# Convolution sums in PSUM, one-hots from columns of biases, and candidates' places spread by ScalarE in a hybrid decoder layer

## The chip, the cores and the metric

The kernel runs on one core of a Trainium2 chip. The metric is device time in microseconds, the median over runs. The kernel before took 3189.76, 3202.34 and 3205.40 us in three runs, median 3202.34 us.

## The reference, cut to what matters

One decoder layer over 1024 tokens of 1024 numbers in f32: attention and a convolution beside each other, then a retrieval among 128 x 128 single-neuron experts (8 heads, 16 experts each per token), then a per-layer embedding behind a gate.

```python
def _token_mixers(xn, ...):                       # attention: left out
    glu = a * jax.nn.sigmoid(gt)
    c = lax.conv_general_dilated(glu, conv_w[:, None, :], window_strides=(1,),
                                 padding=[(CONV_WIDTH - 1, 0)], ...,      # 31 taps, causal
                                 feature_group_count=D_CONV) + conv_b     # 512 channels, each its own
    c = jax.nn.silu(_layernorm(c, conv_ln_g, conv_ln_b))
    ...

def _peer(xn, w_q, sub_keys, expert_u, expert_v):
    q = (xt @ w_q).reshape(N, PEER_HEADS, 2, D_KEY // 2)
    s = jnp.einsum('nhpc,pkc->nhpk', q, sub_keys)
    s_half, i_half = lax.top_k(s, PEER_TOPK)                  # 16 of 128 keys in each half
    cand = (s_half[:, :, 0, :, None] + s_half[:, :, 1, None, :]).reshape(N, PEER_HEADS, 256)
    top_s, top_c = lax.top_k(cand, PEER_TOPK)                 # the places of the best 16 candidates
    i1 = jnp.take_along_axis(i_half[:, :, 0], top_c // PEER_TOPK, axis=-1)
    i2 = jnp.take_along_axis(i_half[:, :, 1], top_c % PEER_TOPK, axis=-1)
    expert = i1 * N_KEYS + i2
    gate = jax.nn.softmax(top_s, axis=-1)
    h = jnp.einsum('td,tkd->tk', xb, expert_u[eb])            # per block of tokens
    act = jax.nn.gelu(h, approximate=False) * gb
    return jnp.einsum('tk,tkd->td', act, expert_v[eb])
```

## The kernel before, in words

**Groups and tiles.** The 1024 tokens are eight tiles of 128, taken in four groups of two. For each group the program goes through norm and projections, attention and convolution (`convolve`), output projection and the next norm, search among the keys, and the choice among candidates. Tiles 0, 1, 6 and 7 find their experts by fetching rows: GpSimd issues an indirect transfer per row number (line 593, six buffers), VectorE multiplies each row of `u` with the token's vector (line 606, 512 rows) and later adds each row of `v` to the sum (line 622, 512 rows). Tiles 2 to 5 go another way: `gate_matrix` builds for each token a matrix of gates over all 128 x 128 experts, writes it to DRAM, and a dense pass (`dense`, lines 700 to 772) runs over every expert with the products split into high and low parts. Eight closing blocks, one for each tile, apply the embedding and the final norm.

**What sets the order.** The program names no order among the engines beyond its data: a scheduler lays out each engine's queue when the program is built, from the dependences, the buffers and the order in the text. The row steps of lines 593, 606 and 622 have no fixed place and are laid between the other steps on GpSimd and VectorE. A queue is then executed in order. The rows of VectorE's queue between two fixed points thus differ from one program to the next.

**The convolution.** A group has four channel tiles of 128 channels by 256 tokens (`c` = 0 to 3). For each, the gated input `glu` is made from two projections (line 335) that lie in PSUM under the tag `lin`. This tag has three buffers of one bank and is shared by all projections, by the transposed convolution output `pc` and by the products of `gate_matrix`. Of the 31 taps, 16 (`SIDE_TAPS`) are products on ScalarE (line 349), which GpSimd adds up in `side` (line 350, 15 additions for each channel tile). The other 15 run on VectorE: line 353 begins the sum `cc` in SBUF, line 356 is 14 multiply-adds on it, and line 357 adds `side`. There are two buffers of `side`, three of `glu` and five of `cc`.

**The candidates' places.** For each tile the places of the 16 chosen candidates (`p16`, 8 heads of 16) are split into the two numbers `i1` and `i2`. VectorE compares every place with 16 constants (line 555, `ge`, bf16, 128 partitions of 2048), where `p16` is read as a broadcast over its last dimension, multiplies and adds up (lines 557 to 566), and compares again with 16 constants (line 569, `eq`). After that, in VectorE's order, come the first norm and the attention of the next group.

**The gate matrices.** Per tile, 32 quads of four tokens. For each quad VectorE makes a one-hot `oa` of the first number times the gate (line 669) out of a difference that TensorE builds in PSUM by two products (`less_keys`, lines 654 and 655). The one-hot `o2` of the second number is made in two ways by turns: in every second quad VectorE compares with `iota`, in the others TensorE builds the difference by the same two products and ScalarE applies an absolute value (line 675) and a ramp `1 - x` cut at zero (line 676). TensorE then multiplies the two for each token (line 679), ScalarE copies the result to a stage (line 680), and SyncE writes a stage of 2 MB to DRAM.

## Time and profile before

| | before |
|---|---|
| three runs | 3189.76, 3202.34, 3205.40 us |
| profiled execution | 3194.15 us |
| span in the trace | 3192.4 us |
| mean granted TensorE clock | 0.940 |
| TensorE (PE) busy | 2774.8 us, 87%, 11839 instructions |
| TensorE weight loads (PEld) | 2011.9 us, 63% |
| VectorE (DVE) busy | 2589.0 us, 81%, 5116 instructions |
| ScalarE (ACT) busy | 1089.5 us, 34%, 1917 instructions |
| GpSimd (POOL) busy | 1539.5 us, 48%, 1268 instructions |
| HBM | 270 GB/s over the span |

The profiled execution is 1.75 us longer than the span of its trace, from the first instruction to the last, and all sums of durations are made within that one execution. Shares of busy time are averages over very different stages: a share of 87% says that TensorE works most of the time, not that it is the limit everywhere. So the stages are looked at one by one, by busy time in stretches of the span. SyncE issues transfers and is not counted as busy. In the views, "idle before, releaser" is the time an engine stood still ahead of an instruction, and what ended it.

### The profile page before, as it was taken

The numbers are of one execution on the slowest core, as the hardware profiler recorded it, in microseconds if no ns is written. First come the engines' busy times: TensorE is split into PE (matmuls) and PEld (weight loads), VectorE is DVE, ScalarE is ACT, GpSimd is POOL, SyncE is SP. The second block draws the span as 40 slices with busy tenths as digits, with TensorE's granted clock in tenths as the row PEclk, the third lists the DMA queues.
The fourth block names the chain that finished last, engine by engine and source line by source line (L and its number), as shares of the span: only waits on it lengthen the run. The fifth ranks groups of instructions, "written<-read, shape, count | busy, mean of one in ns | idle before, by whom it ended". The sixth has DMA issues, their size and how long they took to land. (4 is left out here: it accounts for less than half of the span.)

```text
span 3192.4 us, 36241 instructions
## 1 busy us (share of the span) xinstructions
PE 2774.8 (87%) x11839; PEld 2011.9 (63%) x11839; DVE 2589.0 (81%) x5116; ACT 1089.5 (34%) x1917; POOL 1539.5 (48%) x1268
## 2 busy tenths in 40 slices
PE   6688959968994859995999999999999999999996
PEld 3465625743673545664777777777777777777643
DVE  1728887998899898886888888888889888988861
ACT  2722443363245225662222222222322322222342
POOL 0501585455536521223665565565556566666530
PEclk9898979978997879997999999999999999999998
DMA  4154859718843846989999999999999999999850
GB/s 163 53 177 159 270 193 345 266 53 315 305 164 106 329 152 213 290 259 345 342 347 334 323 343 347 339 337 362 328 341 329 334 354 345 358 330 338 326 209 23
DMA packets 304528, 865.77 MB, mean 271 GB/s; under 512 B 26778, under 2 KB 93746, under 8 KB 304338
## 3 DMA queue, kind: packets, MB, share of 16 engines
q0 software_dynamic: 147456, 536.94, 46.1%
q1 hardware_dynamic: 153616, 323.16, 29.2%
q10 hardware_dynamic: 3266, 3.36, 0.3%
q8 instruction: 93, 1.52, 0.2%
q14 instruction: 97, 0.79, 0.1%
HBM read 819.83 MB, written 43.52 MB: 270 GB/s over the span
## 5 line engine op out<-in xcount | busy, mean ns | idle before, releaser
L593 POOL DMA_INDIRECT u<-in_expert_u_dram,ex x512 | 666.7, 1302 | 825.0 <-DVE hk L606 484.7
L593 POOL DMA_INDIRECT v<-in_expert_v_dram,ex x512 | 676.7, 1322 | 522.9 <-DVE gy L622 377.3
L622 DVE SCALAR_TENSOR_TENSOR gy<-v,ga,gy 128x1024 f32<-128x1024 f32 x512 | 656.7, 1283 | 52.0 <-DMA v<-in_expert_v_dram,ex 42.7
L606 DVE CUSTOM_DVE_ANT_0 u<-u,gxn 128x1024 f32<-128x1024 f32 x512 | 617.7, 1233 | 37.5 <-DMA u<-in_expert_u_dram,ex 36.8
L735 PE MATMUL ph<-xh,uh 128*128 128x512 f32 x1024 | 404.9, 395 | 40.4 <-ACT uh L711 39.6
L737 PE MATMUL ph<-xh,ul 128*128 128x512 f32 x1024 | 406.5, 397 | 25.4 <-DVE ul L713 25.0
L736 PE MATMUL ph<-xl,uh 128*128 128x512 f32 x1024 | 402.3, 393 | 0.0
L753 ACT CAST vh<-v 128x1024 fp32r<-128x1024 f32 x128 | 131.5, 1052 | 759.3 <-PE kept_y L768 517.0
L350 POOL TENSOR_TENSOR side<-side,tap 128x256 f32<-128x256 f32 x240 | 195.9, 818 | 183.8 <-ACT tap L349 170.1
L735 PEld LDWEIGHTS ph<-xh,uh 128*128 128x128 f32 x1024 | 194.5, 190 | 88.4 <-ACT uh L711 48.0
L737 PEld LDWEIGHTS ph<-xh,ul 128*128 128x128 f32 x1024 | 194.1, 190 | 79.4 <-DVE ul L713 39.5
L755 DVE TENSOR_TENSOR vl<-v,vh 128x1024 fp32r<-128x1024 f32 x128 | 154.0, 1222 | 108.7 <-ACT vh L753 105.0
L766 PE MATMUL py<-vh,ah 128*128 128x512 f32 x512 | 204.4, 399 | 40.5 <-ACT ah L745 40.5
L270 PE MATMUL pq<-x2T,w_pq 128*128 128x256 f32 x1024 | 229.8, 383 | 2.7 <-DMA w_pq<-in_peer_wq_dram 1.6
L736 PEld LDWEIGHTS ph<-xl,uh 128*128 128x128 f32 x1024 | 194.6, 190 | 41.2
L270 PEld LDWEIGHTS pq<-x2T,w_pq 128*128 128x128 f32 x1024 | 193.9, 192 | 30.6 <-ACT pqT L480 3.2
L767 PE MATMUL py<-vl,ah 128*128 128x512 f32 x512 | 200.7, 394 | 0.0
L766 PE MATMUL kept_y<-vh,ah 128*128 128x512 f32 x512 | 199.5, 390 | 0.0
L768 PE MATMUL kept_y<-vh,al 128*128 128x512 f32 x512 | 199.5, 390 | 0.0
L767 PE MATMUL kept_y<-vl,ah 128*128 128x512 f32 x512 | 199.3, 389 | 0.0
L768 PE MATMUL py<-vh,al 128*128 128x512 f32 x512 | 198.3, 395 | 0.3 <-DVE al L747 0.3
L711 ACT CAST uh<-u 128x1024 fp32r<-128x1024 f32 x128 | 134.1, 1048 | 110.0 <-DMA u<-in_uT_dram 82.3
(261 smaller groups left out, 4796.5 us busy)
## 6 DMA issues: line engine op xcount, KB each, us to landing
u<-in_uT_dram SPq DMA_DIRECT2D x128, 512.0 KB
v<-in_expert_v_dram SPq DMA_DIRECT2D x128, 512.0 KB
w_pq<-in_peer_wq_dram SPq DMA_DIRECT2D x64, 512.0 KB
gate_d<-stage SPq DMA_DIRECT2D x16, 2048.0 KB
gt<-gate_d SPq DMA_DIRECT2D x64, 512.0 KB
w_o<-in_w_out_dram SPq DMA_DIRECT2D x32, 512.0 KB
w_k<-in_w_qkv_dram SPq DMA_DIRECT2D x16, 512.0 KB
w_q<-in_w_qkv_dram SPq DMA_DIRECT2D x16, 512.0 KB
```

The lines of the kernel that those rows point to most:

```text
L270: nc.tensor.matmul(a, w[:, k, :], xT[:, k, :], start=k == 0, stop=k == KD - 1)
L350: G.tensor_tensor(side, side, m, ALU.add)
L593: d = G.indirect_dma_start(out=e, out_offset=None, in_=table, in_offset=bass.IndirectOffsetOnAxis(ap=index, axis=0))
L606: uses(V.tensor_tensor_reduce(out=e, in0=e, in1=xn, scale=1.0, scalar=0.0, op0=ALU.mult, op1=ALU.add, accum_out=hk[:, k : k + 1]))
L622: uses(V.scalar_tensor_tensor(y, e, act[:, k : k + 1], y, ALU.mult, ALU.add))
L735: nc.tensor.matmul(ph, hi, xh[:, k, :], start=k == 0, stop=False)
L736: nc.tensor.matmul(ph, hi, xl[:, k, :], start=False, stop=False)
L737: nc.tensor.matmul(ph, lo, xh[:, k, :], start=False, stop=k == KD - 1)
L755: V.tensor_tensor(b, v, a.bitcast(F32), ALU.subtract)
L766: nc.tensor.matmul(py, ah[e][:, rows(j)], vh[e][:, half(f)], start=first, stop=False)
L767: nc.tensor.matmul(py, ah[e][:, rows(j)], vl[e][:, half(f)], start=False, stop=False)
L768: nc.tensor.matmul(py, al[e][:, rows(j)], vh[e][:, half(f)], start=False, stop=last_e)
```

## The change

It has three parts. First, the convolution's sum on VectorE is held in a PSUM buffer of the tag `lin` (`cs`, for sums) in place of SBUF, and only the last addition, now line 358, writes the SBUF tile `cc`. Second, ScalarE copies `p16`, broadcast, into the full bf16 tile, and VectorE's two comparisons read that tile and write it in place. Third, a negated copy `i2N` of the transposed second numbers is made, and in every second quad ScalarE builds the difference by four activations over `iota`, one for each token, with a column of `i2N` as bias and the absolute value as function; the two products of TensorE for that quad are gone.

```diff
--- before.py
+++ after.py
@@ -348,13 +348,14 @@
                     m = apool.tile([P, GN], F32, tag="tap", name=f"tap{g}_{c}_{k}", bufs=2)[:, :gn]
                     S.activation(m, xk, AF.Copy, scale=wk)
                     G.tensor_tensor(side, side, m, ALU.add)
-            cc = apool.tile([P, GN], F32, tag="cc", name=f"cc{g}_{c}", bufs=5)[:, :gn]
+            sums = lin(f"cs{g}_{c}")[:, :gn]
             xk, wk = tap(SIDE_TAPS)
-            V.tensor_scalar(cc, xk, wk, cw[:, c, TAPS : TAPS + 1], ALU.mult, ALU.add)
+            V.tensor_scalar(sums, xk, wk, cw[:, c, TAPS : TAPS + 1], ALU.mult, ALU.add)
             for k in range(SIDE_TAPS + 1, TAPS):
                 xk, wk = tap(k)
-                V.scalar_tensor_tensor(cc, xk, wk, cc, ALU.mult, ALU.add)
-            V.tensor_tensor(cc, cc, side, ALU.add)
+                V.scalar_tensor_tensor(sums, xk, wk, sums, ALU.mult, ALU.add)
+            cc = apool.tile([P, GN], F32, tag="cc", name=f"cc{g}_{c}", bufs=5)[:, :gn]
+            V.tensor_tensor(cc, sums, side, ALU.add)
             cT.append(cc)
         return cT
 
@@ -552,7 +553,8 @@
         bcast_k = lambda a: a.unsqueeze(2).to_broadcast(full)
         const = lambda o: cb16[:, o : o + TOPK].unsqueeze(1).unsqueeze(1).to_broadcast(full)
         ge = big("ge")
-        V.tensor_tensor(ge, p16.unsqueeze(3).to_broadcast(full), const(0), ALU.is_ge)
+        S.copy(ge, p16.unsqueeze(3).to_broadcast(full))
+        V.tensor_tensor(ge, ge, const(0), ALU.is_ge)
 
         step = mpool.tile([P, PH, TOPK], BF16, tag="step", name=f"step{nm}")
         V.tensor_copy(step[:, :, 0:1], ix4[:, :, 0, 0:1])
@@ -566,7 +568,8 @@
         total(st, ge)
         V.tensor_tensor(p16, p16, st, ALU.subtract)
         eq = big("eq")
-        V.tensor_tensor(eq, p16.unsqueeze(3).to_broadcast(full), const(2 * TOPK), ALU.is_equal)
+        S.copy(eq, p16.unsqueeze(3).to_broadcast(full))
+        V.tensor_tensor(eq, eq, const(2 * TOPK), ALU.is_equal)
         V.tensor_tensor(eq, eq, bcast_k(ix4[:, :, 1, :]), ALU.mult)
         i2 = mpool.tile([P, PH, TOPK], BF16, tag="i2", name=f"i2{nm}", bufs=ND + 1)
         total(i2, eq)
@@ -646,6 +649,8 @@
             S.copy(d, pt[:, 0:P])
             tr.append(d)
         i2T, gT = tr
+        i2N = gp.tile([P, P], F32, tag="i2N", name=f"i2N{j}", bufs=2)
+        S.activation(i2N, i2T, AF.Copy, scale=-1.0)
         four = [P, 4, NK]
 
         def less_keys(ix, t0, name):
@@ -672,7 +677,8 @@
                     )
                 else:
 
-                    S.activation(o2, less_keys(i2, t0, f"pd2_{j}_{t0}"), AF.Abs)
+                    for e in range(4):
+                        S.activation(o2[:, e, :], iota, AF.Abs, bias=i2N[:, t0 + e : t0 + e + 1])
                     S.activation(o2, o2, AF.Relu, bias=1.0, scale=-1.0)
                 pg = sps(f"pG{j}_{t0}")
                 for e in range(4):
```

The scheduler lays the queues out anew. Three places follow, before and after; a name is buffer, group, channel tile and a running number, so `cc1_3` is the sum of channel tile 3 in group 1, and a number at the end of a tile's name differs between the two programs.

VectorE at the end of the convolution of group 1, before. `r_mix2` is the reciprocal for the norm of group 2, and `u0_31` the row number 31 of `u` for tile 0:

```order
L356 SCALAR_TENSOR_TENSOR cc1_3_2558<-glu1_3_2315,cw_91,cc1_3_2558 128x256
L356 SCALAR_TENSOR_TENSOR cc1_2_2494<-glu1_2_2287,cw_91,cc1_2_2494 128x256
L356 SCALAR_TENSOR_TENSOR cc1_3_2558<-glu1_3_2315,cw_91,cc1_3_2558 128x256
L153 RECIPROCAL r_mix2_2586<-sd_mix2_2584 128x2
L153 RECIPROCAL r_ya1_2788<-sd_ya1_2786 128x2
L356 SCALAR_TENSOR_TENSOR cc1_3_2558<-glu1_3_2315,cw_91,cc1_3_2558 128x256
L334 COPY glu2_0_3862<-last_100 128x30
L606 ISA u0_31_18830,hk0_18734<-u0_31_18830,gxn0_18735 128x1024
```

After:

```order
L356 SCALAR_TENSOR_TENSOR cs1_2_2504<-glu1_2_2295,cw_91,cs1_2_2504 128x256
L356 SCALAR_TENSOR_TENSOR cs1_3_2569<-glu1_3_2323,cw_91,cs1_3_2569 128x256
L356 SCALAR_TENSOR_TENSOR cs1_2_2504<-glu1_2_2295,cw_91,cs1_2_2504 128x256
L356 SCALAR_TENSOR_TENSOR cs1_3_2569<-glu1_3_2323,cw_91,cs1_3_2569 128x256
L358 TENSOR_TENSOR cc1_2_2520<-cs1_2_2504,side1_2_2457 128x256
L358 TENSOR_TENSOR cc1_3_2585<-cs1_3_2569,side1_3_2522 128x256
L153 RECIPROCAL r_mix2_2598<-sd_mix2_2596 128x2
L153 RECIPROCAL r_ya1_2800<-sd_ya1_2798 128x2
L334 COPY glu2_0_3874<-last_100 128x30
L334 COPY glu2_1_3902<-last_100 128x30
L334 COPY glu2_2_3930<-last_100 128x30
L609 ISA u0_36_18885,hk0_18774<-u0_36_18885,gxn0_18775 128x1024
```

Before, the last tap steps of channel tile 3 lie behind `r_mix2`, between row steps; after, both chains of the pair and their last additions come ahead of it, and the rows 31 to 35 have gone earlier.

GpSimd in group 1, before, from the fourth channel tile's first additions (`side1_3`) on; `u0_41` and so on are fetches:

```order
L350 TENSOR_TENSOR side1_3_2511<-side1_3_2511,tap1_3_1_2513 128x256
L593 DMA u0_41_18860<-in_expert_u_dram,ex0_1846 128x1024
L350 TENSOR_TENSOR side1_3_2511<-side1_3_2511,tap1_3_2_2516 128x256
L593 DMA u0_42_18863<-in_expert_u_dram,ex0_1846 128x1024
L350 TENSOR_TENSOR side1_3_2511<-side1_3_2511,tap1_3_3_2519 128x256
L593 DMA u0_43_18866<-in_expert_u_dram,ex0_1846 128x1024
L350 TENSOR_TENSOR side1_3_2511<-side1_3_2511,tap1_3_4_2522 128x256
L593 DMA u0_44_18869<-in_expert_u_dram,ex0_1846 128x1024
```

After, the last additions of the group with the fetches behind them:

```order
L350 TENSOR_TENSOR side1_3_2522<-side1_3_2522,tap1_3_13_2560 128x256
L350 TENSOR_TENSOR side1_3_2522<-side1_3_2522,tap1_3_14_2563 128x256
L350 TENSOR_TENSOR side1_3_2522<-side1_3_2522,tap1_3_15_2566 128x256
L596 DMA u0_42_18903<-in_expert_u_dram,ex0_1852 128x1024
L596 DMA u0_43_18906<-in_expert_u_dram,ex0_1852 128x1024
L596 DMA u0_44_18909<-in_expert_u_dram,ex0_1852 128x1024
```

Before, a fetch stands behind every addition here. After, no fetch lies between `u0_41` and the last side addition: from `side1_0`'s eleventh on, 50 additions stand in a row, and the fetch of row 42 follows them.

ScalarE in the gate matrices, before, at the change from the second of the four tiles to the third (`o2_2_4` is the one-hot of the third tile, tokens 4 to 7; `pG` the gate product):

```order
L680 COPY stage2_0_8074<-pG2_0_8082 128x128x4
L675 ACTIVATE o2_2_4_8093<-pd2_2_4_8094 128x512
L646 COPY gT3_8570<-pgtg3_8568 128x128
L676 ACTIVATE o2_2_4_8093<-o2_2_4_8093 128x512
L680 COPY stage2_0_8074<-pG2_4_8099 128x128x4
L675 ACTIVATE o2_2_12_8123<-pd2_2_12_8124 128x512
L676 ACTIVATE o2_2_12_8123<-o2_2_12_8123 128x512
L680 COPY stage2_0_8074<-pG2_8_8112 128x128x4
L680 COPY stage2_0_8074<-pG2_12_8129 128x128x4
```

After:

```order
L681 ACTIVATE o2_2_4_8131<-cst_85,i2N2_8110 128x128 x2
L686 COPY stage1_3_7978<-pG1_124_8093 128x128x4
L681 ACTIVATE o2_2_4_8131<-cst_85,i2N2_8110 128x128 x2
L686 COPY stage2_0_8112<-pG2_0_8120 128x128x4
L682 ACTIVATE o2_2_4_8131<-o2_2_4_8131 128x512
L681 ACTIVATE o2_2_12_8161<-cst_85,i2N2_8110 128x128 x4
L686 COPY stage2_0_8112<-pG2_4_8137 128x128x4
L682 ACTIVATE o2_2_12_8161<-o2_2_12_8161 128x512
L686 COPY stage2_0_8112<-pG2_8_8150 128x128x4
```

Where one activation over 512 columns of PSUM stood, four over 128 columns stand, with the copies of the gate products between them; the ramp of 512 columns stays as it was.

## Rows read from the trace of the kernel before

**Rows 1.** Busy time by stage, whole span: start:end, length, engines, clock, DMA.
```profile
core 0: us, PE busy (x) PEld busy (x) DVE busy (x) ACT busy (x) POOL busy (x), PEclk, DMA share, GB/s
...
537.00:727.00 190.00, 149.00 (x755) 118.66 (x756) 177.66 (x654) 88.74 (x182) 92.06 (x95) 0.88 0.49 172
...
860.00:1050.00 190.00, 143.60 (x733) 108.09 (x732) 186.36 (x600) 86.51 (x169) 85.99 (x89) 0.88 0.43 151
...
1193.00:1450.00 257.00, 253.28 (x1437) 158.79 (x1436) 219.33 (x357) 152.44 (x270) 67.80 (x63) 0.97 0.82 254
1450.00:1479.00 29.00, 0.00 (x0) 0.00 (x0) 10.54 (x18) 1.42 (x2) 11.53 (x11) 0.53 0.96 350
1479.00:2987.00 1508.00, 1430.47 (x6126) 1153.11 (x6127) 1321.90 (x1738) 404.84 (x521) 895.71 (x647) 0.99 0.93 339
2987.00:3192.40 205.40, 169.17 (x483) 86.81 (x481) 101.91 (x113) 73.67 (x156) 55.82 (x48) 0.90 0.47 172
```

**Rows 2.** One line's instructions: duration in ns, minimum/median/maximum, first and last start.
```profile
engine op xcount: duration ns min/median/max, first and last start us, forms
L622 DVE SCALAR_TENSOR_TENSOR gy<-v,ga,gy x512: 1252/1284/1818, 754.4 to 3077.8; 128x1024 f32<-128x1024 f32 x171
```

**Rows 3.** Timeline of TensorE, start of group 2: start, length; idle before in brackets.
```profile
723.22 1.11 PE L162 MATMUL pt_mix<-cst,xt 128*128 128x128 f32 x4 [35.72 <-ACT xt L286]
```

**Rows 4.** One line's instructions again: the convolution's steps.
```profile
L356 DVE SCALAR_TENSOR_TENSOR cc<-glu,cw,cc x224: 459/834/1028, 93.5 to 1026.6; 128x256 f32<-128x256 f32 x112
...
L357 DVE TENSOR_TENSOR cc<-cc,side x16: 401/412/946, 110.1 to 1028.1; 128x256 f32<-128x256 f32 x16
...
L335 DVE TENSOR_TENSOR glu<-a,sg x16: 410/416/426, 90.8 to 1001.2; 128x256 f32<-128x256 f32 x16
...
L350 POOL TENSOR_TENSOR side<-side,tap x240: 719/787/1797, 92.5 to 1021.8; 128x256 f32<-128x256 f32 x120
```

**Rows 5.** Timelines of VectorE and GpSimd, 105 to 134 us, group 0.
```profile
111.01 10.51 DVE L356 SCALAR_TENSOR_TENSOR cc<-glu,cw,cc 128x256 f32<-128x256 f32 x12
...
105.33 28.79 POOL L350 TENSOR_TENSOR side<-side,tap 128x256 f32<-128x256 f32 x34 [1.64 <-ACT tap L349]
```

**Rows 6.** Groups by line: busy us, mean ns of one | idle before.
```profile
L350 POOL TENSOR_TENSOR side<-side,tap 128x256 f32<-128x256 f32 x240 | 195.9, 818 | 183.8 <-ACT tap L349 170.1
L356 DVE SCALAR_TENSOR_TENSOR cc<-glu,cw,cc 128x256 f32<-128x256 f32 x224 | 162.6, 753 | 1.4
L555 DVE TENSOR_TENSOR ge<-p,cb 128x2048 bf16<-128x2048 bf16 x8 | 18.2, 2281 | 1.1 <-PE pt_p L162 1.1
L561 DVE TENSOR_TENSOR tmp<-ge,step 128x2048 bf16<-128x2048 bf16 x8 | 9.8, 1221 | 0.0
L606 DVE CUSTOM_DVE_ANT_0 u<-u,gxn 128x1024 f32<-128x1024 f32 x512 | 617.7, 1233 | 37.5 <-DMA u<-in_expert_u_dram,ex 36.8
L622 DVE SCALAR_TENSOR_TENSOR gy<-v,ga,gy 128x1024 f32<-128x1024 f32 x512 | 656.7, 1283 | 52.0 <-DMA v<-in_expert_v_dram,ex 42.7 <-DVE gy L622 0.5
```

**Rows 7.** Groups by line, ScalarE; then its timeline in a closing block.
```profile
L675 ACT ACTIVATE o<-pd 128x512 f32<-128x512 f32 x64 | 38.3, 598 | 18.0 <-PE pd L655 17.3 <-DVE o L669 0.7
L676 ACT ACTIVATE o<-o 128x512 f32<-128x512 f32 x64 | 40.4, 631 | 1.8
L680 ACT COPY stage<-pG 128x512 f32<-128x512 f32 x128 | 74.4, 582 | 78.9 <-PE pG L679 76.9 <-issue 2.0
L785 ACT ACTIVATE dg<-cst,r_ple 128x128 f32<-128x128 f32 x8 | 3.2, 399 | 6.5 <-DVE r_ple L153 6.5
...
3164.21 1.14 ACT L792 ACTIVATE x3T<-pt_ple,gains 128x128 f32<-128x128 f32 x4 [2.16 <-PE pt_ple L790]
```

**Rows 8.** Timeline of TensorE within the gate matrices.
```profile
1308.58 1.16 PE L679 MATMUL pG<-oa,o 128*128 128x128 f32 x8
1309.58 0.38 PE L654 MATMUL pd<-ident,i 128*128 128x512 bf16 x1
1309.89 0.38 PE L655 MATMUL pd<-minus,ones 1*128 1x512 bf16 x1
1310.20 1.16 PE L679 MATMUL pG<-oa,o 128*128 128x128 f32 x8
```

**Rows 9.** Groups by line, VectorE: a product from PSUM, one from SBUF.
```profile
L431 DVE SCALAR_TENSOR_TENSOR yc<-pc,mv,ln_g 128x512 f32<-128x512 f32 x8 | 5.7, 727 | 0.0
L432 DVE SCALAR_TENSOR_TENSOR yc<-yc,r_ln,ln_b 128x512 f32<-128x512 f32 x8 | 5.7, 742 | 0.0
```

## The prediction, made before the result was known

> **What bounds the kernel now.** I first cut the span into its stages [rows 1]. In the stretch from 1479 to 2987 us, the dense pass over all experts, TensorE is busy 1430 of 1508 us at a granted clock of 0.99 and the DMA engines 0.93: that is the bound, and the change touches no line of it. Behind it, 2987 to 3192 us, eight closing blocks run one after the other on TensorE. The row gathers, which share VectorE with everything, are used up at 3077.8 us [rows 2], more than 100 us before the end, so they hang on the end only through the order of VectorE's queue. The end is therefore moved by whatever moves the start of the dense pass, microsecond for microsecond. Ahead of it two kinds of stretch remain. In 537 to 727 and 860 to 1050 us VectorE is busy 178 and 186 of 190 us, and TensorE stands still at their end, for 35.72 us before the next group's first transposes [rows 3]: VectorE is the bound there, with gathers, candidate search and convolution in one queue. In 1193 to 1450 us, the gate matrices, TensorE is busy 253 of 257 us, VectorE 219, ScalarE 152. Then come 29 us with nothing on TensorE while the last gate write drains (DMA share 0.96).
>
> Next, what a convolution step costs. The multiply-add of line 356 takes 459 ns at best, 834 at the median and 1028 at most; line 357, which also reads two SBUF tensors, goes from 401 to 946; line 335, which reads one operand from PSUM, stays between 410 and 426 through all 16 [rows 4]. The stretch shows why: 12 multiply-adds take 10.51 us, 0.876 each, while GpSimd's side additions run, and 34 of those take 28.79 us, 0.847 each [rows 5]. They take turns.
>
> **Part 1, sums in PSUM.** The multiply-add keeps glu in SBUF and moves the sum, input and output, to PSUM. No row has this form. Lower end: 0.42 us, line 335's time. Upper end: 1.03 us, the worst contended one of line 356. I take 0.46, the uncontended minimum, since line 335 never stretches. Against the mean of 753 ns [rows 6] that frees 0.29 us on each of 56 multiply-adds per group, with the eight other steps some 17 us of VectorE per group. ScalarE's taps and GpSimd's additions stay: 60 per group at 0.72 us at least, 0.82 on average, so some 49 us of GpSimd per group against 28 us on VectorE. GpSimd is what is late next.
>
> The change also moves steps. The sums take two of the three banks called lin, so the two chains now run in pairs, behind the third GLU, with no gather between them. The gathers go ahead: counted in VectorE's order, 276 rows instead of 250 stand before the first one-hot product, and about as many as before (327 for 323) ahead of the dense pass. 26 rows at 1.3 us [rows 6] are 34 us of VectorE moved from the gate stage into the front.
>
> Group by group. Group 0: the side additions ending at 152 us are no longer slowed, 0.847 to about 0.80 on 50 of them, and the expansions shrink: 7 to 10 us earlier. Group 1 gives this back: its reciprocal for the next norm (r_mix2) now stands behind the last convolution addition, and so behind 50 side additions that start after gather 42, some 41 us where VectorE needs 28. Net 0. Group 2, from the last scaled row to r_mix3: convolution -17, expansions -5.5 (one of three stays there, below), 7 us of other steps of the expansion moved behind, 5 u rows and 8 v rows more, +17: -13 us. Here GpSimd has only the last two side sums, 30 additions or 25 us, left when the 28 us of VectorE's chains begin, so it is covered. Group 3 to r_yc3: convolution -17, expansions -5.5, 2 us of steps moved behind, ten v rows more, +13: -12 us. What moves behind r_mix3 and r_yc3 falls where VectorE waits for TensorE and the weights, so I price it at nothing; without that cover it costs back the 9 us.
>
> **Part 2, places spread by ScalarE.** 16 comparisons fall from 2.28 us to the 1.22 us that the same shape takes with one dense operand [rows 6]: 17 us of VectorE, most of it in the sums above, 2 us more in the stretch before the gates. Added: 16 ScalarE copies of 2048 elements. By line 676's 512 elements in 0.63 us [rows 7] they cost between 0.63 and 2.5 us; I take 1.9. ScalarE is idle half of the time there, but the copy lies in the chain: copy plus comparison is longer than the old comparison by about 0.9 us. VectorE's queue has other candidate work in between; without that 8 times 2 times 0.9, 14 us, comes back.
>
> **Part 3, one-hots from bias columns.** 64 times, one ScalarE pass from PSUM becomes four over 128 columns, and two products of TensorE go. For each pair of token quads TensorE now does three such products of two matmuls, 0.31 us from start to start, so 0.62 each, and two of the gate product at 1.00 [rows 8]: 3.9 us, and 257 us over 64 pairs is 4.0. Without one product it is 3.24: 64 times 0.62, 40 us, is the upper end. ScalarE does 2 times 0.582 + 0.598 + 0.631 = 2.4 us per pair; the four passes at 0.399 each instead of 0.598 make 3.4, or about 3.0 if they overlap as four PSUM passes of that shape do, 1.14 us together [rows 7]. VectorE, with fewer rows to use in the stage (-34 us and more), falls to 3.2. So three engines stand within 10% of each other and wait for each other's two or three buffers. I take 3.56 per pair, 28 us less; lower end 0, if ScalarE takes TensorE's place with waits like those of today. The gate writes and the 29 us of drain stay; the DMA share of 0.82 leaves room, since fewer gathers run beside them.
>
> **Sum.** -13 -12 -2 -28 = -55 us. The profiled execution took 3194.15 us: 3139. It lies 8 us under the median of the runs shown, 3202.34, so 3147 us for a median.
>
> **A price that the trace only half shows.** A product with a PSUM operand, line 431, takes 727 ns for 512 columns, the all-SBUF one behind it 742 [rows 9]: reading PSUM costs nothing extra; writing it is not shown. [...]
>
> **Rivals.**
> 1. ScalarE becomes the gate stage's bound: seven instructions per pair in one queue, the gate copies among them, waits as now. For it: 3.4 us by durations against 3.24 of TensorE. Against it: the overlap. No gain in the stage: 3175. Chance 0.17.
> 2. The front gains nothing: the pairs wait for GpSimd in groups 2 and 3 as in group 1, or the third lin bank holds up the fourth GLU, so that VectorE stands still where it was busy. For it: today's chains fill waits of the attention, the new ones cannot. Against it: the rows moved ahead fill them. 3174. Chance 0.18.
> 3. PSUM accumulation is dear: a chain that reads and writes one bank in place costs more per step than one in SBUF. Since the chains now run as one block with TensorE waiting behind them, each 0.1 us above 0.46 costs 6 us in each of groups 2 and 3, and about half of that in 0 and 1, where GpSimd's 41 us cover it at first. At 1.0 us: 3240, slower. It decides from 0.78 us (no gain) and makes the kernel slower by over 0.5% from 0.87. For it: no row writes PSUM from VectorE. Against it: line 335 and rows 9. Chance 0.08.
> 4. All of it pays: the full 40 us in the gates, group 0's 10 us kept: 3125 or somewhat less. Chance 0.07.
>
> That the change does nothing is excluded: the products and the second SBUF operand are gone from the program.
>
> **How the numbers follow.** The forecast, 3130 to 3165, has 0.50. Rivals 1 and 2 lie at 3174 to 3175; both together would be no change. The range is 3112 to 3196: below it half of rival 4, above it rival 3 and a part of the two failing together. About 0.5%, 16 us, is what a measurement of this kernel can tell from no change. Faster by more than that is under 3186: forecast, rival 4, and most of rivals 1 and 2, 0.80. Same: 0.12. Slower: 0.08, rival 3.
>
> **What would show it.** Line 356 at 0.42 to 0.50 us whatever GpSimd does, side additions at 0.72 to 0.80; VectorE waiting for side at the new line 358 in group 1 and hardly in group 2; the comparisons at 1.2 us; a gate stage near 228 us with 128 instead of 192 products at each of lines 654 and 655 of the kernel before; the dense pass again near 1508 us, starting some 55 us earlier. Line 356 above 0.78 us, a gate stage above 250 us, or a dense pass longer by more than 15 us would prove the step, or the whole, wrong.

## The result and the profile after

The changed kernel takes 3177.19 us, median of 17 runs (3167.28 to 3190.67); the kernel before, run beside it, 3202.88 us (17 runs). The ratio is 0.9924, with an interval of 0.991 to 0.9938: some 24 us faster, where 55 had been forecast. The span of its profiled execution is 3172.8 us, 19.6 under that of before.

Where the difference lies, from the timelines of both profiled executions. A row is the start of an instruction that ends a stage; the last column is what had been forecast for the stage.

| us | before | after | moved by | in its stage | forecast |
|---|---|---|---|---|---|
| norm of group 1 (`r_mix1`) | 274.0 | 278.9 | +4.9 | +4.9 | -7 to -10 |
| norm of group 2 (`r_mix2`) | 422.9 | 442.2 | +19.3 | +14.4 | given back |
| norm of group 3 (`r_mix3`) | 721.8 | 737.5 | +15.7 | -3.6 | -13 |
| conv norm of group 3 (`r_yc3`) | 1046.1 | 1059.6 | +13.5 | -2.2 | -12 |
| first gate product | 1193.7 | 1206.4 | +12.7 | -0.8 | -2 |
| end of the gate products | 1449.9 | 1426.0 | -23.9 | -36.6 | -28 |
| first product of the dense pass | 1479.2 | 1454.9 | -24.3 | -0.4 | 0 |
| its last product | 2991.3 | 2970.7 | -20.6 | +3.7 | 0 |
| end | 3192.4 | 3172.8 | -19.6 | +1.0 | 0 |

So two stories: the front, up to `r_yc3`, was to end 25 us earlier and ends 13.5 us later; the gate matrices gained more than forecast. Behind them the stages differ by 4.3 us in sum, where no change was forecast. By stage, with the columns of [rows 1]:

```profile
core 0: us, PE busy (x) PEld busy (x) DVE busy (x) ACT busy (x) POOL busy (x), PEclk, DMA share, GB/s
...
860.00:1059.60 199.60, 151.20 (x763) 113.31 (x763) 172.06 (x626) 93.71 (x175) 95.79 (x100) 0.88 0.51 173
1206.40:1426.00 219.60, 212.85 (x1307) 145.70 (x1307) 190.55 (x312) 188.82 (x466) 40.34 (x41) 0.97 0.80 241
1426.00:1454.90 28.90, 0.00 (x0) 0.00 (x0) 10.24 (x18) 1.63 (x2) 14.28 (x11) 0.51 0.95 344
1454.90:2970.70 1515.80, 1434.81 (x6146) 1156.41 (x6147) 1325.48 (x1739) 406.62 (x525) 906.90 (x650) 0.99 0.93 339
2970.70:3172.80 202.10, 165.28 (x464) 83.56 (x462) 92.31 (x103) 71.17 (x153) 47.92 (x41) 0.90 0.41 154
```

The gate stage shrank from 256 us to 219.6 us, and TensorE is still busy 212.85 of them, ScalarE now 188.82 (before, 152 us, [rows 1]). The dense pass holds the same work at the same granted clock (0.99, [rows 1]): TensorE is busy 1434.81 us of it, and was 1434.77 between the same two products before.

The groups of instructions by line, answering to [rows 4, 6, 7]; what stands behind the second bar is idle time of the engine ahead of them, and what ended it:

```profile
L350 POOL TENSOR_TENSOR side<-side,tap 128x256 f32<-128x256 f32 x240 | 184.9, 771 | 183.6 <-ACT tap L349 135.1 <-ACT side L346 33.7
L349 ACT ACTIVATE tap<-glu,cw 128x256 f32<-128x256 f32 x240 | 120.5, 507 | 78.9 <-POOL side L350 78.0
L353 DVE TENSOR_SCALAR cs<-glu,cw 128x256 f32<-128x256 f32 x16 | 8.3, 538 | 15.4 <-ACT sg L331 15.4
L356 DVE SCALAR_TENSOR_TENSOR cs<-glu,cw,cs 128x256 f32<-128x256 f32 x224 | 89.2, 480 | 0.0
L358 DVE TENSOR_TENSOR cc<-cs,side 128x256 f32<-128x256 f32 x16 | 6.6, 420 | 52.0 <-POOL side L350 51.9
L556 ACT COPY ge<-p 128x2048 bf16<-128x2048 bf16 x8 | 15.1, 1893 | 2.0 <-DVE p L538 2.0
L557 DVE TENSOR_TENSOR ge<-ge,cb 128x2048 bf16<-128x2048 bf16 x8 | 10.4, 1300 | 3.0 <-ACT ge L556 3.0
L572 DVE TENSOR_TENSOR eq<-eq,cb 128x2048 bf16<-128x2048 bf16 x8 | 9.7, 1216 | 0.0
L681 ACT ACTIVATE o<-cst,i2N 128x128 f32<-128x128 f32 x256 | 85.7, 395 | 0.0
L686 ACT COPY stage<-pG 128x512 f32<-128x512 f32 x128 | 74.3, 580 | 28.7 <-PE pG L685 22.6 <-DMA gate_d<-stage 4.2 <-PE pd L659 0.5
```

Each price came out near its forecast. The multiply-add with its sum in PSUM (line 356) takes 480 ns, against 753 at the mean and 460 forecast; its spread over all 224 is 473 to 484 ns, so it never stretches. The comparisons take 1.30 and 1.22 us (1.22 forecast), ScalarE's copies 1.89 (1.9). The four passes of line 681 take 0.395 each. But a new wait stands in line 358, the last addition: VectorE stood still 51.9 us there until GpSimd had finished `side`, and 15.4 us at line 353, the first step of a sum, until a sigmoid was done. At the same addition before, line 357 there, it was 2.4 us:

```profile
L357 DVE TENSOR_TENSOR cc<-cc,side 128x256 f32<-128x256 f32 x16 | 9.2, 577 | 2.4 <-POOL side L350 2.4
```

That is the front: up to `r_yc3` VectorE's busy time fell from 803.4 to 738.1 us, and its idle time rose from 242.7 to 321.5 us.

### How the wait comes about

VectorE in group 3, from the first sum's start to the reciprocal behind the last:

```profile
1002.11 0.55 DVE L353 TENSOR_SCALAR cs<-glu,cw 128x256 f32<-128x256 f32 x1 [5.79 <-ACT sg L331]
1002.57 11.05 DVE L356 SCALAR_TENSOR_TENSOR cs<-glu,cw,cs 128x256 f32<-128x256 f32 x28
...
1013.62 0.42 DVE L335 TENSOR_TENSOR glu<-a,sg 128x256 f32<-128x256 f32 x1
1013.95 0.74 DVE L358 TENSOR_TENSOR cc<-cs,side 128x256 f32<-128x256 f32 x2
1014.61 0.98 DVE L353 TENSOR_SCALAR cs<-glu,cw 128x256 f32<-128x256 f32 x2
1015.51 11.05 DVE L356 SCALAR_TENSOR_TENSOR cs<-glu,cw,cs 128x256 f32<-128x256 f32 x28
1026.99 0.42 DVE L358 TENSOR_TENSOR cc<-cs,side 128x256 f32<-128x256 f32 x1 [0.44 <-POOL side L350]
1038.90 0.42 DVE L358 TENSOR_TENSOR cc<-cs,side 128x256 f32<-128x256 f32 x1 [11.48 <-POOL side L350]
...
1039.58 0.16 DVE L153 RECIPROCAL r_ya<-sd_ya 128x2 f32<-128x2 f32 x1
```

GpSimd and ScalarE in the same stretch:

```profile
1002.39 2.34 POOL L350 TENSOR_TENSOR side<-side,tap 128x256 f32<-128x256 f32 x3
1014.98 23.89 POOL L350 TENSOR_TENSOR side<-side,tap 128x256 f32<-128x256 f32 x30 [10.26 <-ACT side L346]
...
1014.40 0.91 ACT L346 ACTIVATE side<-glu,cw 128x256 f32<-128x256 f32 x2 [7.93 <-DVE cc L358]
```

And GpSimd in group 3 of the kernel before:

```profile
982.49 18.47 POOL L350 TENSOR_TENSOR side<-side,tap 128x256 f32<-128x256 f32 x20
1001.92 1.89 POOL L350 TENSOR_TENSOR side<-side,tap 128x256 f32<-128x256 f32 x2 [0.96 <-ACT tap L349]
1005.51 17.07 POOL L350 TENSOR_TENSOR side<-side,tap 128x256 f32<-128x256 f32 x19 [1.71 <-ACT tap L349]
```

Read from the bottom: the reciprocal `r_ya` at 1039.58 stands behind the last addition in VectorE's queue. That addition waited 11.48 us, until 1038.90, for GpSimd's 30 additions of the last two channel tiles. These began only at 1014.98, after GpSimd had stood still 10.26 us, because ScalarE could not begin the third `side` (line 346 waits 7.93 us) before the first two additions of line 358, at 1013.95, gave back one of the two buffers. And those stand behind the first pair's 28 multiply-adds, which began only at 1002.57: the second sum could not begin before the last sigmoid (`sg`) had been read out of its bank. Before, the chains ran as each gated input came, and GpSimd's additions ran on with short breaks, 41 additions from 982.49 to 1022.58.

The bank is plainest in group 0, where nothing else is in VectorE's queue:

```profile
113.76 0.43 DVE L335 TENSOR_TENSOR glu<-a,sg 128x256 f32<-128x256 f32 x1 [7.12 <-ACT sg L331]
...
114.48 0.54 DVE L353 TENSOR_SCALAR cs<-glu,cw 128x256 f32<-128x256 f32 x1
121.82 0.55 DVE L353 TENSOR_SCALAR cs<-glu,cw 128x256 f32<-128x256 f32 x1 [6.80 <-ACT sg L331]
122.28 2.05 DVE L356 SCALAR_TENSOR_TENSOR cs<-glu,cw,cs 128x256 f32<-128x256 f32 x5
```

The first gated input was there at 90 us, but the first sum begins at 114.48, right behind the third gated input (line 335 at 113.76), the second at 121.82 after 6.80 us of waiting for the last sigmoid. The sums are written in the text behind all eight projections of the group and take the three lin buffers in turn: the first sum gets the buffer of the third `a`, which the third gated input gives back, the second that of the fourth `gt`, which the last sigmoid gives back.

The end of it, on TensorE, answering to [rows 3]:

```profile
738.90 1.12 PE L162 MATMUL pt_mix<-cst,xt 128*128 128x128 f32 x4 [38.73 <-ACT xt L286]
```

These are the first transposes of group 3, counted from 0 (the heading of rows 3 says 2; it is the same place). TensorE stands still for 38.73 us ahead of them, where it stood 35.72 before: VectorE is faster in each changed step (line 356 takes 480 ns for 753), and is still what TensorE waits for, since it waits for GpSimd (9.43 us at the last addition of group 2).

### The profile page after: what moved, and what is told of

It reads as the page before. It is cut to its first block, busy times and chain, and to the rows that moved or that the text cites. A ratio compares the mean times of both kernels' runs of the same rounds, so it can differ in the third digit from the quotient of the medians.

```text
span 3172.8 us, 36112 instructions
## 1 busy us (share of the span) xinstructions
PE 2723.0 (86%) x11711; PEld 1994.6 (63%) x11711; DVE 2487.8 (78%) x5116; ACT 1154.2 (36%) x2129; POOL 1551.7 (49%) x1268
## 5 line engine op out<-in xcount | busy, mean ns | idle before, releaser
L596 POOL DMA_INDIRECT u<-in_expert_u_dram,ex x512 | 674.1, 1317 | 812.1 <-DVE hk L609 539.4
L596 POOL DMA_INDIRECT v<-in_expert_v_dram,ex x512 | 692.4, 1352 | 494.7 <-DVE gy L625 362.9
L350 POOL TENSOR_TENSOR side<-side,tap 128x256 f32<-128x256 f32 x240 | 184.9, 771 | 183.6 <-ACT tap L349 135.1
## 6 DMA issues: line engine op xcount, KB each, us to landing
gate_d<-stage SPq DMA_DIRECT2D x16, 2048.0 KB, 11.5
```

The costliest lines, as they stand in the source:

```text
L350: G.tensor_tensor(side, side, m, ALU.add)
L596: d = G.indirect_dma_start(out=e, out_offset=None, in_=table, in_offset=bass.IndirectOffsetOnAxis(ap=index, axis=0))
```

## The experiments

Each was timed beside the kernel before. Times are medians; the ratio to the kernel before has its 95% interval.

| run | edit | us | ratio | `r_yc3` at | VectorE's wait for side |
|---|---|---|---|---|---|
| after | all three parts | 3177.2 | 0.9924 (0.991 to 0.9938) | 1059.6 | 51.9 |
| e1_sums | part 1 alone | 3238.1 | 1.0121 (1.0077 to 1.0164) | 1073.5 | 53.0 |
| e2_no_sums | parts 2 and 3 | 3148.6 | 0.9855 (0.9797 to 0.9913) | 1036.0 | 2.6 |
| e5_spread | part 2 alone | 3193.0 | 0.9959 (0.994 to 0.9977) | 1036.4 | 2.6 |
| e6_bias | part 3 alone | 3174.1 | 0.9903 (0.9872 to 0.9934) | 1056.8 | 2.4 |
| e4_taps12 | after, 12 side taps | 3162.0 | 0.9884 (0.9841 to 0.9926) | 1039.6 | 7.2 |
| e7_side3 | after, 3 side buffers | 3149.9 | 0.9834 (0.9796 to 0.9873) | 1045.0 | 23.7 |
| e3_early | after, taps behind each input | 3136.1 | 0.9805 (0.9759 to 0.985) | 1017.3 | 21.0 |
| e9_early_sbuf | e3, sums in SBUF | 3165.0 | 0.9879 (0.9837 to 0.992) | 1054.2 | 2.4 |
| e10_early_sbuf12 | e9, 12 side taps | 3155.2 | 0.9851 (0.9813 to 0.989) | 1040.9 | 0.4 |
| e8_early12 | e3, 12 side taps | 3125.0 | 0.9746 (0.9718 to 0.9774) | 1010.8 | 0.1 |
| e11_early10 | e3, 10 side taps | 3117.2 | 0.9729 (0.968 to 0.9777) | 1005.4 | 0.1 |
| e12_early8 | e3, 8 side taps | 3113.4 | 0.9706 (0.967 to 0.9741) | 991.9 | 0.1 |

The medians of the kernel before, beside these runs, lie between 3200.4 and 3207.7 us, so two medians can differ by up to 7 us for that alone; the ratios are free of it.

Three theories stood against each other: the banks (A), ScalarE's copies in the chain (B), and the row steps that the scheduler moved ahead (C).

### e1_sums: the sums alone

The diff's first hunk (lines 351 to 357) on the kernel before, and nothing else.

> The kernel before with part 1 alone: sums in PSUM buffers of the tag lin, everything else as before. Theory A (banks): of the three lin banks the two sums can take theirs only after the third gated input and the last sigmoid, so the chains start late, hold the two side buffers, and GpSimd's last 30 additions end the group: r_yc of group 3 comes 10 to 20 us later than before (1056 to 1066 us against 1046.1), VectorE waits over 40 us for side at the last addition, the gates take 256 us as before, and the whole is 8 to 20 us longer than before. Theory B (ScalarE's copies): the front of the changed kernel is late because the comparisons now wait for ScalarE; then this kernel's front is earlier than before, r_yc of group 3 at 1030 to 1040 us, and the whole is 5 to 15 us shorter than before.

```profile
L358 DVE TENSOR_TENSOR cc<-cs,side 128x256 f32<-128x256 f32 x16 | 6.6, 419 | 53.0 <-POOL side L350 53.0
L353 DVE TENSOR_SCALAR cs<-glu,cw 128x256 f32<-128x256 f32 x16 | 8.3, 538 | 14.8 <-ACT sg L331 14.8
```

The front is late without a single copy on ScalarE: `r_yc3` at 1073.5, and the wait of 53.0 us is the one of the changed kernel. Theory B falls. The size, 38 us longer than before, lies beyond what A had said (8 to 20): `r_yc3` is 27 us late where 10 to 20 were expected, and the rest, some 13 us, shows in the dense pass of that one profiled execution (1524.9 us against 1512.0), which no step of the theory explains. By itself, part 1 makes the kernel slower.

### e2_no_sums: the other two parts

The changed kernel with the first hunk undone.

> The changed kernel with the sums back in SBUF; the copies and the one-hots from biases stay. Theory A (banks): the front is no longer late, r_yc of group 3 at 1032 to 1046 us, gates about 220 us, the whole 25 to 35 us shorter than the changed kernel (near 3145 us). Theory B (ScalarE's copies): the front stays late, near 1060 us, and the time is that of the changed kernel within 5 us.

```profile
L356 DVE SCALAR_TENSOR_TENSOR cc<-glu,cw,cc 128x256 f32<-128x256 f32 x224 | 163.7, 760 | 1.4
L357 DVE TENSOR_TENSOR cc<-cc,side 128x256 f32<-128x256 f32 x16 | 9.5, 592 | 2.6 <-POOL side L350 2.6
```

28 us shorter than the changed kernel by the medians, 22 by the ratios (the intervals touch), with `r_yc3` at 1036.0: as A had it. Line 357 is the last addition here, and VectorE waits 2.6 us at it. The multiply-add is back at 760 ns, and still this front is the earlier one. But 21 row steps fewer stand ahead of `r_yc3` here (210 for 231), some 27 us of VectorE, so this run does not tell the wait from the rows; e4_taps12 and e7_side3, in which the rows stay, do.

### e5_spread and e6_bias: one part at a time

> The kernel before with part 2 alone, ScalarE's copies ahead of VectorE's comparisons. By the prediction the 16 comparisons fall from 2.28 to 1.22 us and the front gains 5.5 us in each of groups 2 and 3 and 2 us ahead of the gates: r_yc of group 3 at 1034 to 1040 us, the gates as before at 256 us, the whole 5 to 15 us shorter than before. Rival: copy plus comparison, 1.9 and 1.22, is longer than the old comparison and stands in the chain: no gain in the front, the whole within 5 us of before.

> The kernel before with part 3 alone, the one-hots of every second quad from biases. TensorE sets the pace in the gates: the stage from the first to the last gate product falls from 256 to 216 to 224 us, r_yc of group 3 stays at 1046 us within 3, and the whole is 32 to 42 us shorter than before. Rival: ScalarE with its 3.0 to 3.4 us per pair sets the pace or VectorE with its rows: the stage takes 228 us or more, the whole is 28 us shorter at most.

The copies are worth 13 us (0.41%), with `r_yc3` at 1036.4, 9.7 us earlier: the prediction's two times 5.5 and 2. The rival, a chain made longer by copy and comparison, does not show. The one-hots are worth 31 us by the ratio, at the lower edge of what was expected. Two stages missed it: `r_yc3` came at 1056.8, not at 1046, and the gate stage took 229.7 us, not 216 to 224, which is in the rival's range. The profiled execution was the longest of the kernel's five runs (3199.96 us; the others 3165.33 to 3188.43), and its late `r_yc3` is not explained by the edit: no step ahead of the gates is changed, and 204 row steps stand ahead of `r_yc3` as before. The gate stage in four quarters by tile (columns as in [rows 1]):

```profile
core 0: us, PE busy (x) PEld busy (x) DVE busy (x) ACT busy (x) POOL busy (x), PEclk, DMA share, GB/s
...
1203.10:1266.00 62.90, 57.07 (x318) 40.19 (x319) 56.73 (x90) 46.57 (x114) 7.49 (x8) 0.87 0.55 160
1266.00:1326.20 60.20, 55.42 (x326) 37.05 (x325) 45.89 (x75) 46.46 (x118) 12.17 (x13) 0.91 0.87 273
1326.20:1379.80 53.60, 53.60 (x341) 36.55 (x340) 46.19 (x74) 47.32 (x118) 9.37 (x10) 1.00 0.88 262
1379.80:1432.80 53.00, 51.14 (x330) 35.78 (x328) 46.30 (x75) 45.80 (x112) 10.95 (x11) 1.00 0.87 256
```

The last two quarters take the 53 us that they take in the changed kernel (53.6 and 53.3), with TensorE at a granted clock of 1.00; in the first two the clock was 0.87 and 0.91 and they took 62.9 and 60.2. In the changed kernel it was 0.93 and 0.97 there, at 57.5 and 55.2 us. Per pair of quads the last quarters are 53.3 / 16 = 3.33 us at a granted clock of 1.00, between the 3.24 that the prediction worked out for TensorE's products from [rows 8] and the 3.56 that it took. TensorE, busy 53.60 of 53.60 and 51.14 of 53.00 us there, remains the pace; ScalarE, busy 46 of 53 us, does not become it.

### e4_taps12: fewer additions on the side

`SIDE_TAPS = 16` becomes `SIDE_TAPS = 12` in the changed kernel.

> The changed kernel with 12 of the 31 taps on ScalarE and GpSimd instead of 16; 232 row steps ahead of r_yc of group 3, as in the changed kernel (231). Theory A (banks): the last pair's side additions are 22 instead of 30, some 17.5 us, against 38 steps of VectorE at 0.395, 15 us: the wait for side falls from 11.5 us a group to about 3, and r_yc of group 3 comes at 1030 to 1048 us, the whole 10 to 25 us shorter than the changed kernel. Theory C (rows): no gain; VectorE has 64 steps more to do, 25 us in all, and r_yc of group 3 comes 5 to 25 us later than 1059.6.

```profile
L358 DVE TENSOR_TENSOR cc<-cs,side 128x256 f32<-128x256 f32 x16 | 6.5, 414 | 7.2 <-POOL side L350 7.2
```

232 row steps stand ahead of `r_yc3`, VectorE has 64 multiply-adds more, and the front is 20 us earlier (1039.6), the wait down from 51.9 to 7.2 us. The sum closes: 44.7 us less waiting, 64 steps at 0.395 or 25 us more work, 19 or 20 us in all. Theory C, by which nothing waits and the front comes later, falls; GpSimd's additions behind the first pair are what the end of a group waits for. The rows still cost their time: 27 more than before are some 35 us of the front, of which the prediction had priced 30. The whole is 13 to 15 us shorter than the changed kernel, though the intervals overlap.

### e7_side3: a third buffer of side

```diff
-            side = apool.tile([P, GN], F32, tag="side", name=f"side{g}_{c}", bufs=2)[:, :gn]
+            side = apool.tile([P, GN], F32, tag="side", name=f"side{g}_{c}", bufs=3)[:, :gn]
```

> The changed kernel with three buffers of side instead of two; VectorE's order is the same, 231 row steps ahead of r_yc of group 3. If it is the two held buffers that turn the late chains into a pause of GpSimd, GpSimd makes the third channel tile's sum in that pause, 15 additions instead of 30 are left behind the first pair, the wait at the last addition falls from 11.5 us a group to about 0, the sum of them from 52 to under 15 us, r_yc of group 3 comes at 1020 to 1040 us, and the whole is 20 to 40 us shorter than the changed kernel, though the chains begin as late as there. If it is the late chains themselves (the bank alone) or the rows ahead, r_yc of group 3 moves by less than 8 us.

Timelines of GpSimd and VectorE in group 3 of this run:

```profile
1000.16 11.98 POOL L350 TENSOR_TENSOR side<-side,tap 128x256 f32<-128x256 f32 x15 [1.02 <-ACT tap L349]
1012.36 11.97 POOL L350 TENSOR_TENSOR side<-side,tap 128x256 f32<-128x256 f32 x15 [0.21 <-ACT side L346]
...
1007.60 0.74 DVE L358 TENSOR_TENSOR cc<-cs,side 128x256 f32<-128x256 f32 x2
...
1009.15 11.05 DVE L356 SCALAR_TENSOR_TENSOR cs<-glu,cw,cs 128x256 f32<-128x256 f32 x28
...
1024.36 0.42 DVE L358 TENSOR_TENSOR cc<-cs,side 128x256 f32<-128x256 f32 x1 [3.83 <-POOL side L350]
```

GpSimd goes straight from the third side sum (1000.16) to the fourth, where it had stood still 10.26 us, and the last wait is 3.83 us instead of 11.48. The whole is 27 us shorter than the changed kernel. Two numbers missed: the waits add up to 23.7, not under 15, and `r_yc3` came at 1045.0, not by 1040. The chains still begin late, so the buffer mends only a part: both the late chains and the two held buffers count. And 17.6 of the 23.7 us are left in group 1 (6.41 and 11.22), where the third buffer took away next to nothing.

### e3_early: the bank taken in turn

The loop over gated inputs and the loop over taps become one, so each sum is written, and takes its lin buffer, behind its own gated input:

```diff
-        glus = []
+        cT = []
         for c in range(NCT):
...
                 V.tensor_copy(last[:, c, :], glu[:, gn:])
-            glus.append(glu)
-        cT = []
-        for c, glu in enumerate(glus):
             tap = lambda k: (glu[:, k : k + gn], cw[:, c, k : k + 1])
```

> The changed kernel with one edit: each channel tile's taps are written right behind its gated input instead of after all four, so that its sum takes a lin bank in its turn. Theory A (banks): the chains start as early as before the change, GpSimd's pauses between channel tiles go, VectorE's wait for side falls from 52 us to under 20, r_yc of group 3 comes at 1020 to 1038 us, the whole 20 to 40 us shorter than the changed kernel. Theory C (rows): the front is late because 27 more row steps stand ahead of r_yc of group 3 (231 instead of 204), and not because anything waits; here 212 stand ahead, so r_yc would come about 25 us earlier too. Theory B: unchanged.

```profile
L347 POOL TENSOR_TENSOR side<-side,tap 128x256 f32<-128x256 f32 x240 | 189.2, 789 | 168.6 <-ACT tap L346 152.3 <-DVE glu L335 1.1 <-POOL side L347 0.2
L353 DVE SCALAR_TENSOR_TENSOR cs<-glu,cw,cs 128x256 f32<-128x256 f32 x224 | 101.6, 479 | 1.4
L355 DVE TENSOR_TENSOR cc<-cs,side 128x256 f32<-128x256 f32 x16 | 6.7, 420 | 21.0 <-POOL side L347 21.0
```

41 us shorter than the changed kernel. Lines 347, 353 and 355 here are 350, 356 and 358 there. The multiply-add has the same 479 ns; the wait for side is 21.0 us instead of 51.9, and `r_yc3` comes at 1017.3, 42 us earlier. All three lie just outside what was expected: the wait above 20 us, `r_yc3` before 1020, the gain above 40. 212 row steps stand ahead of it here and 231 in the changed kernel; 19 of them at 1.3 us are 25 us of VectorE's time that is also gone from the front, so not all of the 42 us is the wait. At 3136 us this kernel lies 11 us under what had been predicted for the change itself (3147).

### e9_early_sbuf and e10_early_sbuf12: is it the text or the bank?

The same text as e3_early, with the sums back in SBUF (`cc` in place of `sums`), with 16 and with 12 side taps.

> The kernel with taps right behind each gated input (16 on the side), the sums back in SBUF. If what the earlier text gained is the bank taken in turn, it gains nothing where no bank is taken: the time is that of the changed kernel with sums in SBUF and the old text, 3149 us, within 8 us, and sums in PSUM are worth 5 to 20 us against this kernel at 3136. If the text order is worth something by itself, this kernel comes to 3140 us or less, and PSUM is worth nothing.

> The same with 12 taps on the side and 19 on VectorE, sums in SBUF. A step in SBUF takes 0.75 us at the mean while GpSimd adds, so 64 steps more cost VectorE 30 to 48 us less the side additions' 50 us: if PSUM is what makes the smaller side pay, this is 0 to 25 us longer than with 16 taps in SBUF, and 25 to 45 us longer than 3125 us, the same with sums in PSUM. If PSUM does not matter, it is 5 to 15 us shorter than with 16 taps, as it was there.

```profile
L353 DVE SCALAR_TENSOR_TENSOR cc<-glu,cw,cc 128x256 f32<-128x256 f32 x288 | 182.4, 668 | 1.3
L347 POOL TENSOR_TENSOR side<-side,tap 128x256 f32<-128x256 f32 x176 | 156.8, 891 | 195.5 <-ACT tap L346 182.5 <-ACT pT L164 1.6 <-DVE cc L353 0.4
```

The new text gains nothing where no bank is taken: 0.9879 against 0.9855 of e2_no_sums, with intervals that overlap, so e3's gain is the bank's. (It was expected within 8 us of 3149; by the ratios it lies 8 us above, by the medians 16, each taken beside its own runs of the kernel before.) With the bank taken in turn, PSUM is worth 0.74% with 16 taps (0.9879 to 0.9805), some 24 us and more than the 5 to 20 expected, though these two intervals overlap at the edge; the row steps ahead of `r_yc3` are nearly the same, 214 and 212. With 12 taps it is 1.05% (0.9851 to 0.9746), some 34 us, and the intervals lie apart. With 12 taps in SBUF the steps of line 353 take 668 ns at the mean and the side additions 891, against 481 and 817 with sums in PSUM: both are longer. The time was expected longer than or equal to that with 16 taps, and came out 9 us shorter (the intervals overlap): that half of the expectation is not borne out.

### e8_early12, e11_early10, e12_early8: the balance moved

e3_early with `SIDE_TAPS` at 12, 10 and 8.

> The kernel with each channel tile's taps right behind its gated input, and 12 taps on the side instead of 16. The wait for side was 21 us there and GpSimd was still the later of the two: it falls to under 8 us; VectorE has 64 steps more at 0.40 to 0.48, some 28 us over four groups. If GpSimd was what set the end of a group, the whole is 5 to 15 us shorter than with 16 taps (3136 us); if VectorE was, it is 10 to 20 us longer.

> Taps right behind each gated input, sums in PSUM, 10 taps on the side. With 12 VectorE waited no more for side (0.1 us), so VectorE now sets the end of a group and 32 steps more cost it 0.40 to 0.48 us each: 12 to 15 us longer over four groups, of which groups 2 and 3 count in full, so 3125 us becomes 3130 to 3140.

> Taps right behind each gated input, sums in PSUM, 8 taps on the side. From 12 to 10 taps the ratio moved from 0.9746 to 0.9729, less than its interval, though VectorE had 32 steps more: what GpSimd no longer adds pays for them, in row fetches that are issued sooner and row steps that run without a neighbour. If that goes on, the ratio lies between 0.970 and 0.975; if VectorE's steps weigh now, 32 more of 0.40 to 0.48 us bring it to 0.976 to 0.980.

```profile
L347 POOL TENSOR_TENSOR side<-side,tap 128x256 f32<-128x256 f32 x176 | 143.7, 817 | 182.2 <-ACT tap L346 171.4
L353 DVE SCALAR_TENSOR_TENSOR cs<-glu,cw,cs 128x256 f32<-128x256 f32 x288 | 128.7, 481 | 1.2
L355 DVE TENSOR_TENSOR cc<-cs,side 128x256 f32<-128x256 f32 x16 | 6.7, 416 | 0.1
```

With 12 taps the wait at the last addition is gone (0.1 us) and 11 us more are gained by the medians, 19 by the ratios, with intervals that overlap. The expectation for 10 taps was wrong: it was to be slower, since VectorE no longer waited, and was not. From 12 taps to 8 GpSimd makes 64 additions fewer and VectorE 64 steps more, and the front still ends earlier, at 991.9 us against 1010.8. Some 15 us of VectorE's time there may be rows: 199 row steps stand ahead of `r_yc3` with 8 taps and 211 with 12; what pays for the steps was not taken apart. With 8 taps the kernel takes 3113 us, a ratio of 0.9706, within the first of the two ranges expected. It is the fastest of all runs, though its interval overlaps those of 12 and 10 taps; against 16 taps (0.9805) the intervals lie apart.

## Why the prediction was wrong

**What held.** The bound: the dense pass took 1515.8 us against 1512.1, so the end moved with its start. The prices: 0.48 us for 0.46, 1.30 and 1.22 for 1.22, 1.89 for 1.9, 0.395 for 0.399. Part 2, alone, gave the 13 us of its terms. Part 3 was forecast at -28 and gave -36.6 in the trace and 31 by itself: the direction and the bound (TensorE) held, and the term was too cautious: 219.6 us over 64 pairs are 3.43 us per pair for the 3.56 taken. A part of this lies in its own working. It put VectorE at 3.2 us per pair, but 219 us less 34 over 64 pairs are 2.9, and 2.98 was measured; ScalarE took 2.95, TensorE 3.33. So the other two had more room beside TensorE than "within 10%"; that they therefore waited less for each other is argued, not tested.

**The step that failed** is in Part 1, group by group: "Here GpSimd has only the last two side sums, 30 additions or 25 us, left when the 28 us of VectorE's chains begin, so it is covered." The 30 additions were right (23.89 us). But the 28 us are both pairs' chains; the first pair's run before those additions may begin, since both side buffers are held until that pair's two last additions. Only the second pair's 12 us (0.98 of first steps and 11.05 of multiply-adds) run beside them, and 11.5 us of VectorE's standing still is what is left over, in each group: 11.48 in groups 0, 1 and 3, 9.43 in group 2. The prediction had seen that the chains go in pairs, and that GpSimd would be late in group 1; it put that down to the fetches in group 1's queue, and did not ask what the two buffers of `side` allow. For group 1 the fetches may have their part, since the third buffer of e7_side3 did not help there. The late start failed beside it: the prediction had the chains begin behind the third gated input, and the second sum of a pair began only behind the last sigmoid, 15.4 us of waiting in sum.

**The sum by it.** The forecast was -55 against the profiled execution, and -19.6 was measured. Groups 2 and 3 were to give 25 us and gave 5.8; groups 0 and 1 were to give nothing in sum and cost 19.3: 38.5 us lost. The stretch ahead of the gates gave 0.8 instead of 2, the gates 8.6 more than forecast, and 4.3 were lost behind them: -55 + 38.5 + 1.2 - 8.6 + 4.3 = -19.6. In groups 2 and 3 the work came out as forecast or better: VectorE's busy time fell by 18.5 and 15.4 us, where 13 and 12 had been forecast with the rows counted in. What was put at nothing is the idle time, which grew by 15.0 and 13.1 us. The wait for `side` makes 8.0 and 11.9 of that. In group 2 VectorE also waited longer for fetched rows of `u`, 26.3 us instead of 12.4; no run takes this apart from the wait for `side`. In group 1 five more rows stand ahead of `r_mix2` (36 for 31), some 6 us that the prediction's "Net 0" does not count.

**The rivals.** The second, that the front gains nothing because the pairs wait for GpSimd in groups 2 and 3 too or the third lin bank holds VectorE up, is what happened, by its first mechanism. The bank held VectorE up as well (15.4 us at line 353), but at the second sum and not at the fourth gated input, which in group 3 stands right behind the first pair's chains without a wait. The rival was given 0.18 and 3174 us; measured were 3177. That this is so near is partly luck: the front did not stay level but ended 13.5 us later, and the gates gave 8.6 us more. The first (ScalarE bound in the gates) and the third (dear accumulation in PSUM) did not come. A step in PSUM took 0.473 to 0.484 us, 480 ns at the mean, and the shortest in SBUF 459 [rows 4]: 21 ns more, on 224 steps 4.7 us by estimate. The contention itself did end with part 1: the SBUF form went up to 1.03 us beside GpSimd [rows 4], the PSUM form in the changed kernel never past 0.484. In group 3 the first pair's 28 steps, during most of which GpSimd stands still, and the second pair's 28, beside its additions, take 11.05 us alike.

**Open.** The three parts do not add up: alone they are worth +1.21, -0.41 and -0.97%, in sum -0.17, and together -0.76%. In e1_sums and e6_bias the last group or the dense pass of the one profiled execution was 8 to 18 us longer for no step that differs; whether this is the order of the row fetches or chance was not tried. The intervals of the three parts (0.4, 0.2 and 0.3 to either side) leave room for a part of the gap to be chance.

## What to carry to other kernels

In this kernel a buffer of the rotating pool was given not by size but by its turn: a sum that lives long in a pool of short-lived projections began when the projection that held its buffer had been read out (in group 0 at 114.48 and 121.82 us, with the first gated input there at 90), and with each sum written behind its own input VectorE's wait for `side` fell from 51.9 us to 21.0. So look at what frees each buffer, and write the sum where its input is made. Two engines shared a job here over a pair of buffers, and the faster one's gain counted only as far as the buffers let the other work meanwhile: the last wait of group 3 was 11.48 us with two buffers of `side` and 3.83 with three. After making one side faster, move the split (here from 16 side taps to 8, 23 us by the medians) and ask what it will be waiting for.

## What was not expected of the hardware

In the changed kernel a multiply-add of VectorE that accumulates in place in PSUM took 480 ns for 256 columns (473 to 484 over all 224), GpSimd's additions beside it or not, 21 ns more than the shortest in SBUF (459, [rows 4]); two such chains laid alternately went at 0.395 us a step (28 in 11.05 us).
